# Head norms scaled by ScalarE out of the projection's bank, mixer outputs and K0 one step later in the order, the tanh table loaded behind the sines

## The chip, the core and the metric

The kernel runs on one core of a Trainium2 chip. The metric is the device time of one execution, in microseconds (us); the median of three runs counts. Five engines work in parallel, each through its own queue in order: TensorE (PE in the rows; its weight loads are PEld), VectorE (DVE), ScalarE (ACT), GpSimd (POOL) and SyncE (SP), which issues the DMA transfers. SBUF is the memory on the chip; PSUM holds the banks into which TensorE accumulates.

## What is computed

Two transformer blocks on 256 tokens of width 1024. The change touches the first block only: its input projections, and the two mixers that run beside them, a state space mixer and a sparse attention whose heads are normalized.

```python
def first_block(x, ...):
    h = rmsnorm(x, norm1_g[l])
    hp = h @ w_in[l]
    y_ssm = s5_mixer(hp[..., :o1], ...)
    y_nsa = nsa_mixer(hp[..., o1:o2], hp[..., o2:o3], hp[..., o3:o4], ...)
    gate = jax.nn.sigmoid(hp[..., o4:].reshape(bsz, s, N_MIXERS, D_MODEL))
    merged = gate[..., 0, :] * (y_ssm @ w_proj_ssm[l]) + gate[..., 1, :] * (y_nsa @ w_proj_nsa[l])
    x = x + merged @ w_out[l]
    ...                        # a feed-forward layer
def nsa_mixer(q, kv, ...):
    q = rmsnorm(q.reshape(bsz, s, G, HG, d), q_norm_g)      # 8 heads of 64, each with its own norm
    ks = rmsnorm(kv[1, 0], k_norm_g[1])                     # 2 of the 4 key heads
    kw = rmsnorm(kv[2, 0], k_norm_g[2])                     # the other 2
    ...
def s5_mixer(u, ...):
    bu = einsum(u, bbar); x = scan(abar, bu)                # complex states, 32 groups of 64
    y = einsum(x, c) + d * u; yg = gelu(y)
    return yg * sigmoid(yg @ w_glu + b_glu)
```

The second block (retention, latent attention, feed-forward layers) follows and is not changed.

## The kernel before

Tokens are two tiles of 128 (t = 0, 1), on the partitions of a projection's result. `block1_proj(t)` is a generator: it multiplies the unnormalized input `x32` by the weights of u, q, kvb, kva and mg one after the other, in PSUM banks (mm, acc0 to acc3), and each result is scaled by the token's norm factor `r` when it leaves its bank. q of tile t lies in bank acc{t}, kva of tile t in bank acc{2+t}. `head_norm` then squares the copy on ScalarE, sums each head's squares on VectorE, takes the power of -0.5 on GpSimd (`rsqrt`, line 332) and multiplies the copy by it on GpSimd (line 847). Its transposes come later, with the functions in `todo`, through the two banks `tr`.

The state space mixer goes in eight steps of `ssm_states(m)`, called s0 to s7: each is matmuls into acc0 and acc1, an evacuation by VectorE (line 754), and after a yield a scan (line 764), two products, and two combinations on GpSimd (lines 768, 769) into one of the three buffers X0 to X2. Line 731 on makes the tables that the steps need, from m = 1 on with GpSimd. Four outputs `ssm_out(i)`, called o0 to o3, read K0, the products `sC` and two of the X buffers, and end in a gelu on ScalarE and VectorE (lines 799, 554 to 557). `ssm_setup`, the generator `st`, makes the tables: sines (ScalarE's Sin table, then line 909's Tanh), the products `sC` (lines 627 to 629), K0 (32 matmuls of 32 columns, copied by line 698) and last the second half of `sC`.

The attention mixer `nsa_chain` compresses keys and values (64 small matmuls from buffers `XT`, which line 920 fills), and then goes through four pairs of heads (lines 1063 to 1084 and `nsa_values`).

What runs when is set in two places. `order` calls the generators D (projections of both tiles, one step apart), S (the mixer's steps), N (the attention) and st in an order written out by hand; `ssm_steps` holds the order of the mixer's steps as a string. From that program order a scheduler places the instructions on each engine's queue, where they then run in order; a wait for another engine's result stops the queue.

Of the kernel before, what the change touches and what calls it, by code (L numbers as in the profile page):

```python
# [12 lines left out]
AF = mybir.ActivationFunctionType  # L13
ALU = mybir.AluOpType
PSUM = bass.MemoryType.PSUM
P = 128
# [161 lines left out]
class Prog:  # L178
# [5 lines left out]
    def __init__(self, ctx, tc, ins, out):  # L184
        self.tc, self.nc, self.i, self.out, self.ctx = tc, tc.nc, ins, out, ctx
        self.dbg = {}
        ec = ctx.enter_context
        self.cp = ec(tc.tile_pool(name="cp", bufs=1))
        self.wp = ec(tc.tile_pool(name="wp", bufs=1))
        self.xp = self.np = None  # L190
        self.mrs = [None, None]
        self.un = 0
        self.hp = ec(tc.tile_pool(name="hp", bufs=1))
        self.pp = ec(tc.tile_pool(name="pp", bufs=1, space=PSUM))
        self.have, self.subs, self.copies, self.left = {}, {}, {}, {}
        keys = lambda *names: [key for name in names for key in UNITS if key[0] == name]
        mg = keys("mg")
        self.raws, self.seen, self.rn = keys("u", "q", "kvb", "kva") + mg[:2], set(), 0
        order = mg[2:]

        self.then = {mg[1]: mg[2]}
        self.ahead = dict(zip(order, order[1:]))
        self.n = 0
# [356 lines left out]
    def ssm_setup(self, pool, np_):  # L560
        nc, v, g = self.nc, self.nc.vector, self.nc.gpsimd
# [3 lines left out]
        def sb(s, tag):  # L565
            if list(s) != [P, 16]:
                return self.sb(pool, s, tag)
            used[0] += 1
            return small[:, used[0] - 1, :]
# [26 lines left out]
        sn, cs = e1[:, 1], e1[:, 0]  # L596
        yield
        self.sincos(pool, th, sn, cs, 16)

        def sq(o, x):  # L600
            t = self.sb(pool, [P, 2, 16], "q1", bufs=2)
            v.tensor_mul(t, x, x)
            v.tensor_sub(o[:, 0], t[:, 0], t[:, 1])
            v.scalar_tensor_tensor(o[:, 1], x[:, 0], 2.0, x[:, 1], op0=ALU.mult, op1=ALU.mult)
# [10 lines left out]
        abr, abi, nr = sb([P, 16], "abr"), sb([P, 16], "abi"), sb([P, 16], "nr")  # L615
# [167 lines left out]

    def ssm_steps(self, pool):
        st = [self.ssm_states(pool, m) for m in range(8)]
        for x in "s0 s1 s0 s2 s1 o0 s3 s2 s4 s3 o1 s5 s4 s6 s5 o2 s7 s6 s7 o3".split():
            i = int(x[1])
            if x[0] == "o":
                self.ssm_out(pool, i)
            else:  # L790
                next(st[i], None)
            yield
# [42 lines left out]
            nc.gpsimd.memset(self.XT[i][:, 256:], 0.0)  # L835
            nc.gpsimd.tensor_copy(self.XT[i][:, 256:272], pe[:, i, :])

    def head_norm(self, pool, src, n):
        nc, v = self.nc, self.nc.vector
        sq = self.sb(pool, [P, 2, 256], "ns1", bufs=2).rearrange("p a k -> p (a k)")  # L840
        nc.scalar.activation(sq[:, :n * 64], src, AF.Square, scale=0.125)
        ms = self.sb(pool, [P, 8], "nms", bufs=2)
        v.tensor_reduce(ms[:, :n], sq[:, :n * 64].rearrange("p (h d) -> p h d", h=n), axis=mybir.AxisListType.X, op=ALU.add)
        v.tensor_scalar_add(ms[:, :n], ms[:, :n], EPS)
        r = self.rsqrt(pool, ms[:, :n], n, tag="nr")
        s3 = src.rearrange("p (h d) -> p h d", h=n)
        nc.gpsimd.tensor_mul(s3, s3, r.unsqueeze(2).to_broadcast([P, n, 64]))

    def proj_then(self, out, name, n, hT, todo, after=1, raw=False):

# [7 lines left out]
    def block1_proj(self, sp, pool, t):  # L858

        nc, v = self.nc, self.nc.vector  # L860
        sq = self.sb(self.b1, [P, UW], "g8k", bufs=2)[:, :1024].rearrange("p (c t) -> p c t", c=8)
# [9 lines left out]
        r = self.rs[t] = self.norm_stats(pool, self.xT[t], f"rstd{t}", sq)  # L871
# [9 lines left out]
        pm = self.ps("mm")  # L881
# [8 lines left out]
        pm = self.ps(f"acc{t}")  # L890
        yield from self.proj_then(pm, "q", 0, x32, todo, 0, True)
        q = self.sb(pool, [P, 512], "q", bufs=2)
        nc.scalar.mul(q, pm, r)
        self.head_norm(pool, q, 8)

        def q_rest(q=q):
            x = flip(q, 4).rearrange("p (c t) -> p c t", c=4)
# [5 lines left out]
        pm = self.ps("mm")  # L903
# [19 lines left out]
        pm = self.ps(f"acc{2 + t}")  # L923
        yield from self.proj_then(pm, "kva", 0, x32, todo, 0, True)
        k = self.sb(pool, [P, 512], "q", bufs=2)[:, :256]
        nc.scalar.mul(k, pm[:, :256], r)
        nc.scalar.mul(self.V[:, t, :], pm[:, 256:], r)
        self.head_norm(pool, k, 4)

        def k_rest(k=k):  # L930
            pt = flip(k, 2)
# [8 lines left out]
        pm = self.ps("mm")  # L940
# [7 lines left out]
        for n in range(1, 4):  # L948
            pm = self.ps("mm")
# [198 lines left out]
    def order(self, D, st, S, N, sp):  # L1148

        next(D)  # L1150
        self.w1 = [self.sb(self.b1, [P, 16, P], "g8k", bufs=2) for _ in (0, 1)]
        for k in range(4):
            next(D)
            next(st)
            if k == 1:
                for i in (0, 1):
                    self.nc.sync.dma_start(self.w1[i], self.i["cw1"][i])
        next(S)
        next(D)
        next(st, None)  # L1160
        next(S)
        next(D)
        for k in range(2):
            for x in (S, N, S):
                next(x)
            next(st, None)
            next(D)
        while D is not None:
            for _ in range(3):
                next(S, None)  # L1170
                next(N, None)
            if next(D, 1) == 1:
                D = None
        self.weave(S, N)
# [474 lines left out]
```

## Time and profile before

| | |
|---|---|
| median of three runs | 1421.97 us (1418.32 to 1424.17) |
| the profiled execution | 1418.17 us, its span 1416.0 us |
| TensorE busy | 98% of the span |
| VectorE, ScalarE, GpSimd busy | 66%, 53%, 9% |
| mean granted TensorE clock | 0.995 of 2.4 GHz |

The span runs from the first to the last instruction; what lies around it makes up the rest of the execution's time. The first block takes about the first 220 us. Ends of matmuls are modelled in the profile, so that "busy" there means that TensorE had work, not that it was at its peak. A wait is idle time of an engine, put down to the instruction that came last.

### The profile page before, as it was taken

Reading aid. Unit: us, or ns where it says so; the run is one execution under the profiler, and the core shown is the slowest. Engines: PE = TensorE matmul, PEld = TensorE weight load, DVE = VectorE, ACT = ScalarE, POOL = GpSimd, SP = SyncE. Lnnn points to the kernel's source line nnn. Section 1 sums busy time; section 2 is a strip of 40 time slices with the busy share of each in tenths; the row PEclk is TensorE's granted clock in tenths of the full one; section 3 lists DMA queues with packets and bytes.
Section 4 is the critical chain, followed back from the end, with each engine's and each line's share of the span. In section 5 each row is a group of like instructions: output and inputs, shape, how many; then the busy total and the mean of one; then the engine's idle time right before and its main releaser. Section 6 shows DMA issues by size and latency. Waiting matters only on the chain.

```text
span 1416.0 us, 18450 instructions
## 1 busy us (share of the span) xinstructions
PE 1381.4 (98%) x6690; PEld 1107.7 (78%) x6690; DVE 928.5 (66%) x1990; ACT 749.3 (53%) x1647; POOL 129.8 (9%) x147
## 2 busy tenths in 40 slices
PE   7999999999999999999999999999999999999997
PEld 3656787888877888889877888878888887788886
DVE  6887687755676555587688565576555596865553
ACT  3345556544665444465366454465444576744442
POOL 1644100800000000011000000000000000000000
PEclk9998999999999999999999999999999999999999
DMA  9222355755545555435354555545555252565540
GB/s 359 87 91 68 109 208 180 251 189 180 178 179 192 194 179 180 152 104 194 127 199 158 182 211 188 181 146 208 188 198 179 81 180 81 187 212 197 186 149 30
DMA packets 39114, 238.62 MB, mean 169 GB/s; under 512 B 5744, under 2 KB 7024, under 8 KB 13424
## 3 DMA queue, kind: packets, MB, share of 16 engines
q1 hardware_dynamic: 39024, 237.45, 48.0%
q8 instruction: 52, 0.85, 0.2%
q14 instruction: 38, 0.31, 0.1%
HBM read 236.39 MB, written 1.05 MB: 168 GB/s over the span
## 4 chain that ended last, share of the span: by engine, by line
PE 78%; DVE 11%; ACT 3%; issue 3%; DMA 3%; POOL 2%; SPq 0%; POOLq 0%; DVEq 0%; ACTq 0%
PE mm L222 44%; PE acc L222 29%; PE tr L226 4%; DVE wl L263 3%; DMA raw<-in_wts_dram 3%; DVE s L375 2%; DVE hTl L390 1%; ACT wh L262 1%; PE tr L222 1%; DVE xT L430 1%; DVE tb L764 1%; ACT hTh L389 0%; POOL rr L332 0%; POOL nr L332 0%; DVE xT L426 0%
## 5 line engine op out<-in xcount | busy, mean ns | idle before, releaser
L263 DVE TENSOR_TENSOR wl<-raw,wh 128x512 fp32r<-128x512 f32 (+2 forms) x852 | 536.6, 681 | 255.6 <-ACT wh L262 254.9
L262 ACT CAST wh<-raw 128x512 fp32r<-128x512 f32 (+2 forms) x852 | 461.9, 606 | 303.5 <-PE mm L222 152.1
L222 PE MATMUL mm<-wh,hTl 128*128 128x512 f32 (+2 forms) x1056 | 406.1, 389 | 0.5 <-DVE hTl L390 0.5
L222 PE MATMUL mm<-wh,hTh 128*128 128x512 f32 (+2 forms) x1024 | 398.7, 390 | 2.3 <-ACT hTh L389 2.1
L222 PE MATMUL mm<-wl,hTh 128*128 128x512 f32 (+2 forms) x1024 | 393.6, 385 | 0.1
L222 PEld LDWEIGHTS mm<-wh,hTl 128*128 128x128 f32 x1056 | 198.9, 189 | 42.3 <-issue 3.4
L222 PEld LDWEIGHTS mm<-wh,hTh 128*128 128x128 f32 x1024 | 192.9, 188 | 42.9 <-ACT hTh L389 5.0
L222 PEld LDWEIGHTS mm<-wl,hTh 128*128 128x128 f32 x1024 | 193.0, 189 | 36.6 <-issue 0.7
L222 PE MATMUL acc<-wh,ffhh 128*128 128x512 f32 x480 | 196.4, 409 | 0.0
L222 PE MATMUL acc<-wh,ffhl 128*128 128x512 f32 x480 | 188.8, 393 | 0.0
L222 PE MATMUL acc<-wl,ffhh 128*128 128x512 f32 x480 | 188.7, 393 | 0.0
L449 ACT ACTIVATE ffs<-mm,rstd 128x256 f32<-128x256 f32 x88 | 41.7, 473 | 138.7 <-PE mm L222 137.9
L450 DVE SCALAR_TENSOR_TENSOR ffh<-mm,rstd,ffs 128x256 f32<-128x256 f32 x88 | 42.4, 482 | 104.1 <-ACT ffs L449 102.3
L222 PEld LDWEIGHTS acc<-wh,ffhl 128*128 128x128 f32 x480 | 90.2, 188 | 20.2
L222 PEld LDWEIGHTS acc<-wl,ffhh 128*128 128x128 f32 x480 | 90.6, 189 | 16.7
L222 PEld LDWEIGHTS acc<-wh,ffhh 128*128 128x128 f32 x480 | 90.3, 188 | 16.4
L332 POOL TENSOR_TENSOR rr<-ms,mhalf 128x1 f32<-128x1 f32 x12 | 7.1, 589 | 772.3 <-DVE ms L412 771.7
L222 PE MATMUL acc<-wh,mx 128*128 128x512 f32 x160 | 53.9, 403 | 0.1
L325 ACT CAST ffhh<-tr 128x256 fp32r<-128x256 f32 (+1 forms) x104 | 41.6, 400 | 20.7 <-PE tr L226 20.7
L326 DVE TENSOR_TENSOR ffhl<-tr,ffhh 128x256 fp32r<-128x256 f32 (+1 forms) x104 | 47.7, 459 | 6.1 <-ACT ffhh L325 5.3
L226 PE MATMUL tr<-idn,ffh 128*128 128x128 f32 x240 | 43.2, 272 | 0.0
L226 PEld LDWEIGHTS tr<-idn,ffh 128*128 128x128 f32 x240 | 32.2, 140 | 13.5 <-DVE ffh L450 0.6
(402 smaller groups left out, 1380.8 us busy)
## 6 DMA issues: line engine op xcount, KB each, us to landing
raw<-in_wts_dram SPq DMA_DIRECT2D x194, 1024.0 KB, 4.9
raw<-in_wts_dram SPq DMA_DIRECT2D x18, 768.0 KB, 4.2
raw<-in_wts_dram SPq DMA_DIRECT2D x4, 576.0 KB, 3.7
wl<-in_wts_dram SPq DMA_DIRECT2D x2, 1024.0 KB, 12.0
g8k<-in_cw_dram SPq DMA_DIRECT2D x2, 1024.0 KB, 10.0
wh<-in_wts_dram SPq DMA_DIRECT2D x2, 1024.0 KB, 9.1
memT<-in_memT_dram SPq DMA_DIRECT2D x4, 512.0 KB, 3.6
raw<-in_wts_dram SPq DMA_DIRECT2D x4, 256.0 KB, 5.7
```

Source lines behind the costliest of these rows:

```text
L222: self.nc.tensor.matmul(out, l, r, start=start, stop=stop, **kw)
L226: self.nc.tensor.transpose(out, src, self.idn[:n, :n])
L262: self.copies[key] = nc.scalar.copy(wh[:, s:s + h], raw[:, s:s + h]).ins
L263: self.subs[key] = nc.vector.tensor_sub(wl[:, s:s + h], raw[:, s:s + h], wh[:, s:s + h].bitcast(F32)).ins
L325: self.nc.scalar.copy(hi, src)
L326: self.nc.vector.tensor_sub(lo, src, hi.bitcast(F32))
L375: nc.vector.tensor_reduce(s8, sq.rearrange("p c t -> p t c"), axis=mybir.AxisListType.X, op=ALU.add)
L390: nc.vector.scalar_tensor_tensor(lo[:, c, :], xT[:, c, :], g[:, c:c + 1], hi[:, c, :].bitcast(F32), op0=ALU.mult, op1=ALU.subtract)
L430: nc.vector.scalar_tensor_tensor(xT[:, cc, :], pt[:, c * P:(c + 1) * P], gain[:, cc:cc + 1], xT[:, cc, :], op0=ALU.mult, op1=ALU.add)
L449: nc.scalar.activation(s, pm[:, :256], AF.Silu, scale=rstd)
L450: nc.vector.scalar_tensor_tensor(h, pm[:, 256:], rstd, s, op0=ALU.mult, op1=ALU.mult)
L764: v.tensor_tensor_scan(fb[:, n], RD.rearrange("p j t -> p (j t)"), fa[:, n], 0.0, op0=ALU.mult, op1=ALU.add)
```

## The change

Four things. `head_norm` now gets the bank: the Square reads it with the token's factor in its scale (`r8`), VectorE multiplies the heads' factors by `r` in a new row, and ScalarE writes each head out of the bank with one multiplication of 64 columns, in place of the copy and of GpSimd's multiplication. In the string of `ssm_steps` o0, o1 and o2 stand one step later. In `order` one `next(st, None)` is gone, so that K0 and the second half of `sC` each come one call later. And a one-column Tanh behind the sines brings in its table there.

```diff
@@ -596,6 +596,7 @@
         sn, cs = e1[:, 1], e1[:, 0]
         yield
         self.sincos(pool, th, sn, cs, 16)
+        self.table(AF.Tanh)
 
         def sq(o, x):
             t = self.sb(pool, [P, 2, 16], "q1", bufs=2)
@@ -783,7 +784,7 @@
 
     def ssm_steps(self, pool):
         st = [self.ssm_states(pool, m) for m in range(8)]
-        for x in "s0 s1 s0 s2 s1 o0 s3 s2 s4 s3 o1 s5 s4 s6 s5 o2 s7 s6 s7 o3".split():
+        for x in "s0 s1 s0 s2 s1 s3 o0 s2 s4 s3 s5 o1 s4 s6 s5 s7 o2 s6 s7 o3".split():
             i = int(x[1])
             if x[0] == "o":
                 self.ssm_out(pool, i)
@@ -835,16 +836,18 @@
             nc.gpsimd.memset(self.XT[i][:, 256:], 0.0)
             nc.gpsimd.tensor_copy(self.XT[i][:, 256:272], pe[:, i, :])
 
-    def head_norm(self, pool, src, n):
+    def head_norm(self, pool, out, src, n, r, r8):
+
         nc, v = self.nc, self.nc.vector
         sq = self.sb(pool, [P, 2, 256], "ns1", bufs=2).rearrange("p a k -> p (a k)")
-        nc.scalar.activation(sq[:, :n * 64], src, AF.Square, scale=0.125)
+        nc.scalar.activation(sq[:, :n * 64], src, AF.Square, scale=r8)
         ms = self.sb(pool, [P, 8], "nms", bufs=2)
         v.tensor_reduce(ms[:, :n], sq[:, :n * 64].rearrange("p (h d) -> p h d", h=n), axis=mybir.AxisListType.X, op=ALU.add)
         v.tensor_scalar_add(ms[:, :n], ms[:, :n], EPS)
-        r = self.rsqrt(pool, ms[:, :n], n, tag="nr")
-        s3 = src.rearrange("p (h d) -> p h d", h=n)
-        nc.gpsimd.tensor_mul(s3, s3, r.unsqueeze(2).to_broadcast([P, n, 64]))
+        nr = self.rsqrt(pool, ms[:, :n], n, tag="nr")
+        v.tensor_scalar_mul(nr, nr, r)
+        for h in range(n):
+            nc.scalar.mul(out[:, 64 * h:64 * h + 64], src[:, 64 * h:64 * h + 64], nr[:, h:h + 1])
 
     def proj_then(self, out, name, n, hT, todo, after=1, raw=False):
 
@@ -890,8 +893,9 @@
         pm = self.ps(f"acc{t}")
         yield from self.proj_then(pm, "q", 0, x32, todo, 0, True)
         q = self.sb(pool, [P, 512], "q", bufs=2)
-        nc.scalar.mul(q, pm, r)
-        self.head_norm(pool, q, 8)
+        r8 = self.sb(pool, [P, 1], "rn8", bufs=2)
+        v.tensor_scalar_mul(r8, r, 0.125)
+        self.head_norm(pool, q, pm, 8, r, r8)
 
         def q_rest(q=q):
             x = flip(q, 4).rearrange("p (c t) -> p c t", c=4)
@@ -923,9 +927,8 @@
         pm = self.ps(f"acc{2 + t}")
         yield from self.proj_then(pm, "kva", 0, x32, todo, 0, True)
         k = self.sb(pool, [P, 512], "q", bufs=2)[:, :256]
-        nc.scalar.mul(k, pm[:, :256], r)
         nc.scalar.mul(self.V[:, t, :], pm[:, 256:], r)
-        self.head_norm(pool, k, 4)
+        self.head_norm(pool, k, pm[:, :256], 4, r, r8)
 
         def k_rest(k=k):
             pt = flip(k, 2)
@@ -1157,7 +1160,6 @@
                     self.nc.sync.dma_start(self.w1[i], self.i["cw1"][i])
         next(S)
         next(D)
-        next(st, None)
         next(S)
         next(D)
         for k in range(2):
```

Three places show how the queues change. The first is VectorE, at the head norms of q (lines 842 to 844 before; `L845`, `L846`, `L848` in the changed file, whose numbers are two to three higher there). `nms` and `nr` are the heads' sums and factors, first of tile 0 and then of tile 1, and the `sC` rows are the products of the mixer's set-up. Before:

```order
L844 TENSOR_SCALAR nms_374<-nms_374 128x8
L627 TENSOR_TENSOR sC_403<-ns_79_319,small_152 128x512
L628 TENSOR_TENSOR ta_425<-V_142,small_152 128x512
L627 TENSOR_TENSOR sC_403<-ns_79_319,small_152 128x512
L629 TENSOR_TENSOR sC_403<-sC_403,ta_425 128x512
L628 TENSOR_TENSOR ta_429<-V_142,small_152 128x512
L627 TENSOR_TENSOR sC_403<-sC_403,small_152 128x512
L629 TENSOR_TENSOR sC_403<-sC_403,ta_429 128x512
L627 TENSOR_TENSOR sC_403<-sC_403,small_152 128x512
L843 TENSOR_REDUCE nms_414<-ns_104_412 128x8
L844 TENSOR_SCALAR nms_414<-nms_414 128x8
L754 TENSOR_TENSOR ta_443<-acc_110_433,cst_341 128x2x128
```

And now:

```order
L628 TENSOR_TENSOR sC_414<-ns_80_321,small_152 128x512
L848 TENSOR_SCALAR nr_98_380<-nr_98_380,rstd_19_125 128x8
L629 TENSOR_TENSOR ta_445<-V_142,small_152 128x512
L628 TENSOR_TENSOR sC_414<-ns_80_321,small_152 128x512
L630 TENSOR_TENSOR sC_414<-sC_414,ta_445 128x512
L629 TENSOR_TENSOR ta_449<-V_142,small_152 128x512
L628 TENSOR_TENSOR sC_414<-sC_414,small_152 128x512
L630 TENSOR_TENSOR sC_414<-sC_414,ta_449 128x512
L628 TENSOR_TENSOR sC_414<-sC_414,small_152 128x512
L845 TENSOR_REDUCE nms_426<-ns_107_424 128x8
L846 TENSOR_SCALAR nms_426<-nms_426 128x8
L848 TENSOR_SCALAR nr_109_429<-nr_109_429,rstd_51_201 128x8
```

Two rows came in, each of which reads GpSimd's power: one behind the first `sC` product, one between tile 1's sums and the evacuation of s0 (`ta<-acc`).

The second place is ScalarE at the same norms. acc_56 and acc_82 (acc_83 now) are the banks acc0 and acc1 with q of tile 0 and tile 1; mm is the bank of kvb. Before:

```order
L893 ACTIVATE q_370<-acc_56_212,rstd_19_125 128x512
L841 ACTIVATE ns_94_372<-q_370 128x512
L893 ACTIVATE q_410<-acc_82_330,rstd_51_201 128x512
L681 COPY sB_76_299<-tr_391 128x4x128
L681 COPY sB_76_299<-tr_397 128x4x128
L841 ACTIVATE ns_104_412<-q_410 128x512
L758 COPY RD_40_169<-small_152 128x2x127
L908 ACTIVATE q_454<-mm_380,rstd_19_125 128x256
L909 ACT_TABLE_LOAD
```

And now:

```order
L843 ACTIVATE ns_96_375<-acc_56_212,rn_95_373 128x512
L850 ACTIVATE q_372<-acc_56_212,nr_98_380 128x64 x8
L843 ACTIVATE ns_107_424<-acc_83_332,rn_106_422 128x512
L682 COPY sB_77_301<-tr_402 128x4x128
L682 COPY sB_77_301<-tr_408 128x4x128
L850 ACTIVATE q_421<-acc_83_332,nr_109_429 128x64 x8
L759 COPY RD_40_169<-small_152 128x2x127
L912 ACTIVATE q_474<-mm_391,rstd_19_125 128x256
L913 ACTIVATE gts_143<-mm_391,hr_472 128x24
```

The last read of acc0 and acc1 is now that of the eight pieces, which need the `nr` rows above; the table load has gone from this place to behind the sines.

The third place is VectorE between the first two pairs of heads (lines 1069 to 1077 before, 1072 to 1080 now), at the evacuation of s6 (line 754 before, 755 now; it needs a `cst` table of GpSimd). Before:

```order
L1077 TENSOR_TENSOR ns_255_1130<-ns_255_1130,nsm_1117 128x256
L1070 TENSOR_TENSOR nsm_1121<-nsm_1121,gts_143 128x4
L765 TENSOR_TENSOR ta_1092<-tb_1093,cst_1073 128x512
L754 TENSOR_TENSOR ta_1246<-acc_271_1236,cst_1227 128x2x128
L754 TENSOR_TENSOR tb_1247<-acc_271_1236,cst_1227 128x2x128
L754 TENSOR_TENSOR ta_1246<-acc_272_1237,cst_1227 128x2x128
L754 TENSOR_TENSOR tb_1247<-acc_272_1237,cst_1227 128x2x128
L1077 TENSOR_TENSOR ns_256_1135<-ns_256_1135,nsm_1121 128x256
```

And now:

```order
L1080 TENSOR_TENSOR ns_258_1156<-ns_258_1156,nsm_1143 128x256
L1072 RECIPROCAL nsm_1147<-nsm_1147 128x4
L766 TENSOR_TENSOR ta_1078<-tb_1079,cst_1059 128x512
L1073 TENSOR_TENSOR nsm_1147<-nsm_1147,gts_143 128x4
L767 TENSOR_TENSOR tb_1079<-tb_1079,cst_1059 128x512
L1080 TENSOR_TENSOR ns_259_1161<-ns_259_1161,nsm_1147 128x256
L263 TENSOR_TENSOR wl_1363<-raw_1361,wh_1362 128x512
L755 TENSOR_TENSOR ta_1272<-acc_274_1262,cst_1253 128x2x128
```

The second product of the pair now stands ahead of the evacuation of s6. On TensorE, of what the text below speaks of, K0's 32 matmuls moved from ahead of s1 to behind the compression's matmuls, s3 moved from behind tile 1's k transposes to ahead of them, and o0 from ahead of mg's first matmuls to behind these transposes; s0 stands where it stood.

## Rows read from the trace of the kernel before

**Rows 1.** The page: busy times (part 1), GpSimd's one-column powers (part 5).

```profile
PE 1381.4 (98%) x6690; PEld 1107.7 (78%) x6690; DVE 928.5 (66%) x1990; ACT 749.3 (53%) x1647; POOL 129.8 (9%) x147
...
L332 POOL TENSOR_TENSOR rr<-ms,mhalf 128x1 f32<-128x1 f32 x12 | 7.1, 589 | 772.3 <-DVE ms L412 771.7
```

**Rows 2.** TensorE's waits, 0 to 160 us: us in total, times, longest.

```profile
PE tr L226 <- DVE ns L1077: 2.3, 2, 1.8
PE tr L226 <- POOL q L847: 1.8, 1, 1.8
PE tr L222 <- DVE qT L900: 1.6, 1, 1.6
PE tr L226 <- DVE s L994: 0.8, 1, 0.8
...
PE acc L222 <- DVE tb L754: 0.4, 1, 0.4
```

**Rows 3.** Busy times by stretch; behind them the granted clock and DMA.

```profile
92.00:146.00 54.00, 49.97 (x317) 34.89 (x317) 45.21 (x147) 31.49 (x99) 21.58 (x25) 0.91 0.24 76
```

**Rows 4.** Timeline of TensorE: start, duration, line, operation, count [idle before <-releaser].

```profile
45.04 1.16 PE L222 MATMUL acc<-uT,sB 32*128 32x128 f32 x16
...
53.94 0.76 PE L222 MATMUL tr<-sC,PT 128*32 128x32 f32 x64 [1.57 <-DVE qT L900]
```

**Rows 5.** Timeline of VectorE at the q norms.

```profile
37.17 1.23 DVE L627 TENSOR_TENSOR sC<-ns,small 128x512 f32<-128x512 f32 x1
...
43.74 0.68 DVE L627 TENSOR_TENSOR sC<-sC,small 128x512 f32<-128x512 f32 x1
44.35 0.67 DVE L843 TENSOR_REDUCE nms<-ns 128x8 f32<-128x512 f32 x1
45.05 0.30 DVE L844 TENSOR_SCALAR nms<-nms 128x8 f32<-128x8 f32 x1
```

**Rows 6.** Timeline of GpSimd: table products and the powers of the q norms.

```profile
39.98 2.09 POOL L733 TENSOR_TENSOR cstt<-BA 128x256 f32<-128x256 f32 x2
42.03 2.10 POOL L332 TENSOR_TENSOR nr<-nms,mhalf 128x8 f32<-128x8 f32 x1
...
45.43 1.65 POOL L332 TENSOR_TENSOR nr<-nms,mhalf 128x8 f32<-128x8 f32 x1
...
55.54 1.21 POOL L733 TENSOR_TENSOR cstt<-BA 128x256 f32<-128x256 f32 x2
```

**Rows 7.** Timeline of ScalarE: behind the sines, the table load, copies of 64 columns.

```profile
27.93 0.69 ACT L884 ACTIVATE q<-mm,rstd 128x512 f32<-128x512 f32 x1 [6.66 <-PE mm L222]
...
50.95 1.28 ACT L909 ACT_TABLE_LOAD   x1
...
54.28 0.42 ACT L920 COPY XT<-tr 64x64 f32<-64x64 f32 x2 [0.81 <-DVE XT L920]
```

**Rows 8.** Timeline: a k norm's power, s4 on TensorE, a cast on ScalarE.

```profile
69.86 4.33 POOL L332 TENSOR_TENSOR nr<-nms,mhalf 128x4 f32<-128x4 f32 x1 [2.91 <-DVE nms L844]
...
90.10 1.79 PE L222 MATMUL acc<-uT,sB 32*128 32x128 f32 x16 [0.41 <-DVE tb L754]
...
90.86 0.62 ACT L262 CAST wh<-raw 128x512 fp32r<-128x512 f32 x1 [1.96 <-DMA raw<-in_wts_dram]
```

**Rows 9.** VectorE's wait at s6 (timeline), and three stretches as in rows 3.

```profile
128.48 0.42 DVE L754 TENSOR_TENSOR ta<-acc,cst 128x256 f32<-128x256 f32 x1 [1.78 <-POOL cst L734]
...
130.00:132.00 2.00, 1.26 (x8) 1.20 (x9) 2.00 (x8) 0.81 (x3) 0.29 (x1) 0.86 0.00 0
132.00:134.00 2.00, 2.00 (x8) 1.16 (x8) 2.00 (x10) 2.00 (x10) 1.99 (x3) 0.50 0.00 0
134.00:136.00 2.00, 2.00 (x16) 1.46 (x14) 0.66 (x2) 0.39 (x3) 2.00 (x3) 0.78 0.00 0
```

**Rows 10.** Timeline of TensorE at the start.

```profile
7.15 2.05 PE L222 MATMUL mm<-raw,hTl 128*128 128x512 f32 x2 [7.15 <-DMA raw<-in_wts_dram]
...
13.28 3.60 PE L222 MATMUL mm<-wh,hTl 128*128 128x512 f32 x8
```


## The prediction

> **What bounds the kernel now.** I read the page's busy shares first: TensorE is busy for 1381.4 us of the 1416.0 us span [rows 1], so a change on other engines is worth only what it takes from, or adds to, TensorE's waits and its clock. The list of TensorE's waits over the first 160 us, where all the edits lie, comes next. Besides the first load it holds five groups that the edits touch: 2.3 us on `L1077` (two, the longest 1.8), 1.8 on `L847`, 1.6 on `L900`, 0.8 on `L994`, 0.4 on `L754` [rows 2]. Last I read busy time and granted clock by stretch: from 92 to 146 us the mean clock is 0.91 [rows 3], that is 54 × 0.09 × 2 = 9.7 us at 1.2 GHz where the rest runs at 2.4. So the most that perfect order could give is some 7 us of waits and 5 us of clock. Half a per cent of the time, about what a measurement of this kernel can tell from no change, is 7.1 us.
>
> **The change, part by part.** *The norms.* Before, ScalarE copied a projection out of its bank in one instruction (`L893`), and GpSimd scaled the copy (`L847`). Now the Square reads the bank, VectorE scales the 8 (or 4) factors by `r`, and ScalarE takes each head out of the bank by a multiplication of its own. Two things follow that the diff doesn't show.
>
> First, VectorE gets a row (`L848`) that waits for GpSimd's power, and its queue stops there. For token tile 0 it stands one row behind the first `sC` product, with seven products of K0's set-up, the other tile's reduce and the evacuation of s0 behind it. VectorE comes to it at 37.17 + 1.23 = 38.4. GpSimd began that power at 42.03 [rows 5, 6], behind table products that it must still do first. Between 38.4 and 42.03 it worked through some 3.5 products at about 1.05 us each, against VectorE's, of which one took 1.23 instead of 0.61. Alone it takes 0.60 for one [rows 6], so with VectorE at rest the power starts near 40.6, takes the 1.65 of the second power, and with its signal and the scaling row VectorE goes on at about 42.6 (estimates from these rows, as all that follows). Seven products at 0.61 (from 43.74 to 44.35) lead to 46.9, the reduce at 0.70 to 47.6, the small row to 47.8, the second power at 1.65 to 49.45, its `L848` to 49.7 [rows 5, 6].
>
> Second, the bank is held until its last head is out. The q projections of the tiles lie in acc0 and acc1, and s0 of the state space part writes the same two banks. Before, they were free by then, and TensorE ran s0 at 45.04 without waiting [rows 4]. Now the second matmul of s0 needs the eight pieces of tile 1, which start at 49.7. The nearest row is the pair of 64x64 copies out of a bank, 0.42 for two [rows 7], so eight take 1.7. That leads to 51.5 with the signal: **TensorE waits 6.5 us more at s0**, and everything behind is in order on TensorE.
>
> *A page on that price.* The Trainium skill, ScalarE: Activation LUTs, section "What ACT_TABLE_LOAD costs", gives an activation with one pointer operand 280 ns and 0.833 ns an element, and an overlap of 93 ns between two; eight of 64 would be 2.0 us, an estimate from that page. It speaks against cutting one instruction into eight, and by it the wait would be 6.8. No row here has just this form, so the copies' 0.21 stands.
>
> The bounds of the 6.5: the power of one column takes 0.589 in the mean [rows 1], so two powers can't save more than 2.1 (4.4 us); the first power took 2.10, and two such and slower pieces add 1.3 (7.8 us).
>
> *K0 one step later, the tanh table earlier.* K0's matmuls waited 1.57 us for `L900` [rows 4], which stood behind the 1.28 us table load on ScalarE [rows 7]. The load goes to 21.3 us, where ScalarE idles 6.66 us [rows 7], and costs nothing; without that cover it would cost 1.28 on the u copy. K0 now runs behind the compression's matmuls. **−1.6**; nothing takes the place of this wait, since the copy `L908` and the transposes that need it both move with s0.
>
> *The k norms.* `L847` made TensorE wait 1.8 us because the power in front of it took 4.33 us beside a busy VectorE [rows 2, 8]. Now the k norm of tile 0 starts as soon as its bank is done, VectorE stands still for its power, and 64 matmuls of the compression and K0 lie before its transposes: **−1.8**.
>
> *Outputs one step later.* s3 now comes ahead of o0, so that s3 and s4 no longer stand back to back. There s4 waited 0.41, and its 16 matmuls took 1.79 instead of 1.16 [rows 4, 8]: **−1.0**. Before, the chain to `L994` stood on ScalarE behind a cast that waited 1.96 us for its load [rows 8]; now that cast comes after it: **−0.8**. Between 124 and 131 us the second `L1077` stood behind an `L754` that waited 1.78 us for a GpSimd table [rows 9]; now it stands ahead of it: **−1.8**, the longest of these waits [rows 2].
>
> *The clock.* After the first load, 7.15 us of idling, the first 8 matmuls of 512 columns took 6.1 us (7.15 to 13.28), the next 8 took 3.60 [rows 10]: 2.5 us lost. After the wait of 1.8 us on `L1077` the granted clock was 0.86, 0.50 and 0.78 in three stretches of 2 us [rows 9], 3.4 us at 1.2 GHz, 1.7 lost. A wait of 6.5 us lies between these, nearer the first: **+2.0** (0 to 2.5). With the wait on `L1077` goes the fall behind it: **−1.7**. The first fall of that stretch, 9.7 − 3.4 = 6.3 us long, stays: it doesn't hang on the wait on `L1077`, which comes behind it.
>
> *Unseen.* VectorE has five more rows and four stops. The nearest danger is tile 1's k norm, whose transposes come about 0.6 us behind its heads, with o0's `sC` behind the same stop: **+1.0** (0 to 2.7, the difference of a power at 4.33 and one at 1.65 [rows 6, 8]).
>
> **The sum**: 6.5 − 1.6 − 1.8 − 1.0 − 0.8 − 1.8 + 2.0 − 1.7 + 1.0 = **+0.8 us**. The profiled execution took 1418.17 (span 1416.0, and 2.2 around it) and would go to 1419.0. It lies 3.8 under the median of the three runs, 1421.97, so the forecast for a median is 1422.8, no change that can be measured.
>
> **The rivals.** *VectorE doesn't catch up (slower).* Stopped four times in order, it stays behind from s0 on; the waits on `L994` and `L1077` and the fall of the clock, which all come from its being late, stay (0.8 + 1.8 + 1.7 = 4.3), and the power of tile 1's k norm runs at 4.33 against VectorE's products (2.7 in place of 1.0). Sum: 0.8 + 4.3 + 1.7 = 6.8, or 1428.8. For it: VectorE was busy 45.21 of 54 us there [rows 3], and the change takes no work from it. Against: s3's scans come earlier than before. It decides from 6.3 us beyond the sum on, where the loss passes 7.1.
> A page beside it: the Trainium skill, SBUF — State Buffer, section "SBUF: two separate sides", says that a VectorE instruction with two inputs in SBUF and a GpSimd one hold the port that they share in turn, each for a whole instruction. The 4.33 us power agrees with that [rows 8]; by this rule the case is the nearer, the more of VectorE's products lie beside a norm's power.
>
> *The wait at s0 isn't there (faster).* If the heads were out of acc1 before 45, only the removed waits would count: 0.8 − 6.5 − 2.0 = −7.7, or 1414.3. That needs both powers done 6 us sooner; GpSimd's in-order table products [rows 6] speak against it.
>
> *The order around 107 us changes the first fall too.* Its 6.3 us cost 3.1. Without it the time is 1419.7. The new order there puts wide matmuls between narrow ones, at places that the rows can't weigh.
>
> **How the numbers follow.** The sum's case gets 0.62, with a range of its own from 1418 to 1426 (the bounds of the wait, of the clock and of the unseen, taken partly together). Lateness gets 0.18, no wait 0.08, the lost fall 0.12. Slower by over 0.5% is half of the lateness case (0.09) and the far tail of the sum's (0.04), 0.13; faster by over 0.5% is most of the no-wait case (0.06) and a little of the lost fall (0.02), 0.08; the rest, 0.79, is within 0.5%. The range 1415.5 to 1430 reaches to both neighbours and leaves out most of the no-wait case and the tail beyond lateness.
>
> **What would show it.** In the trace after: TensorE waiting 4.4 to 7.8 us on ScalarE's head pieces at s0, near 45; VectorE idle about 4 us before its first `L848`, with GpSimd as releaser; a lower clock right behind 51; no wait on `L900` or on the k heads of tile 0; transposes near 75 about 3 us later than before, and those after 131 level with before. I am wrong if TensorE passes 45 without a wait, if VectorE isn't stopped by the power, or if the stretch from 92 to 146 us keeps its waits or gets new ones.

## The result and the profile after

The changed kernel takes 1434.57 us in the median (1432.29 to 1436.29), the kernel before 1421.6 in the same rounds: a ratio of 1.0097 [1.0082, 1.0112], 13 to 14 us slower, and outside the predicted range. The profiled execution took 1435.47 us with a span of 1433.5, 17.5 more than the span of before; that one lay some 3 us under its median, so the traces differ by more than the medians. TensorE runs the same 6690 instructions by tile and shape; what differs is waits and clock. In the lists of the changed kernel line numbers are up to 3 higher (`L1077` is now `L1080`, `L994` is `L997`, `L1036` is `L1039`).

TensorE's waits over the first 160 us of the changed kernel, to be held against [rows 2]:

```profile
engine line waited for: us in total, times, longest us
PE mm L222 <- DMA raw<-in_wts_dram: 7.9, 1, 7.9
PE acc L222 <- ACT q L850: 5.4, 1, 5.4
PE tr L226 <- DVE cs L1039: 1.9, 1, 1.9
PE tr L222 <- DVE kT L939: 1.9, 1, 1.9
PE tr L222 <- POOL cst L735: 1.9, 1, 1.9
PE tr L226 <- ACT ns L1078: 1.6, 1, 1.6
PE tr L226 <- DVE ns L1080: 1.3, 1, 1.3
PE acc L222 <- ACT sB L682: 0.8, 1, 0.8
PE tr L226 <- DVE s L997: 0.6, 1, 0.6
```

The waits on `L900`, on the k heads and on `L754` are gone; the wait at s0 is there; and five of 1.3 us and more stand in the list behind it, of which before had only `ns` on VectorE at such a length. Next the granted clock by stretch (busy time and rows of each engine, then clock, DMA share and GB/s), where before had 1.00, 0.91 [rows 3] and 1.00:

```profile
45.00:92.00 47.00, 38.95 (x262) 23.79 (x261) 31.75 (x71) 17.99 (x53) 19.25 (x26) 0.85 0.17 58
92.00:146.00 54.00, 46.68 (x276) 30.61 (x275) 44.27 (x140) 25.55 (x77) 16.06 (x18) 0.88 0.22 72
146.00:160.00 14.00, 13.55 (x79) 9.29 (x77) 12.21 (x37) 9.08 (x28) 6.62 (x9) 0.87 0.29 95
```

That is 47 × 0.15 × 2 + 54 × 0.12 × 2 + 14 × 0.13 × 2 = 30.7 us at 1.2 GHz, where before had 9.7 [rows 3]. TensorE does half as much in such a microsecond, so 21.0 more of them cost 10.5. Added up over stretches of 1 us the two kernels have 30.7 and 10.2, in four falls (50 to 58, 74 to 82, 118 to 130, 142 to 150 us) against two. **So between these two executions 10 of the 17.5 us are clock, 7.6 are TensorE's waits, and 0.8 is the first load**: 18.4, about what is to be explained. Between the medians the share of the clock is smaller, some 4 us of 13, because the profiled execution of before had a higher clock than most of its others; the part "Kernel or execution?" below has the numbers.

The place of the s0 product in the changed kernel, on TensorE (start, duration, instructions, idle time before and its releaser), on ScalarE, on VectorE and on GpSimd:

```profile
46.83 0.48 PE L222 MATMUL acc<-uT,sB 32*128 32x128 f32 x2 [0.80 <-ACT sB L682]
52.71 2.07 PE L222 MATMUL acc<-uT,sB 32*128 32x128 f32 x14 [5.40 <-ACT q L850]
54.71 5.04 PE L222 MATMUL acc<-raw,hTl 128*128 128x512 f32 x8
...
74.04 0.44 PE L222 MATMUL tr<-g8k,XT 128*48 128x128 f32 x2 [1.85 <-POOL cst L735]
```
```profile
43.97 1.75 ACT L850 ACTIVATE q<-acc,nr 128x64 f32<-128x64 f32 x8 [11.06 <-DVE nr L848]
50.91 1.75 ACT L850 ACTIVATE q<-acc,nr 128x64 f32<-128x64 f32 x8 [3.65 <-DVE nr L848]
```
```profile
43.65 0.23 DVE L848 TENSOR_SCALAR nr<-nr,rstd 128x8 f32<-128x8 f32 x1 [4.88 <-POOL nr L332]
50.65 0.23 DVE L848 TENSOR_SCALAR nr<-nr,rstd 128x8 f32<-128x8 f32 x1 [1.76 <-POOL nr L332]
72.06 0.58 DVE L848 TENSOR_SCALAR nr<-nr,rstd 128x4 f32<-128x4 f32 x1 [2.25 <-POOL nr L332]
72.56 0.45 DVE L924 COPY XT<-tr 64x64 f32<-64x64 f32 x2
73.03 0.75 DVE L904 SCALAR_TENSOR_TENSOR qT<-tr,g,qT 128x512 fp32r<-128x512 f32 x1
```
```profile
69.75 0.73 POOL L770 TENSOR_TENSOR X<-tb,ta 128x256 f32<-128x256 f32 x1
70.43 0.62 POOL L733 TENSOR_TENSOR cst<-BA 128x256 f32<-128x256 f32 x1
71.01 1.02 POOL L332 TENSOR_TENSOR nr<-nms,mhalf 128x4 f32<-128x4 f32 x1
```

VectorE stops 4.88, 1.76 and 2.25 us for the powers, the eight pieces come out of the bank in 1.75, and TensorE loses 0.80 + 5.40 at s0. The eight matmuls behind take 5.04 us; before, at the full clock, they took 3.70:

```profile
46.13 3.70 PE L222 MATMUL acc<-raw,hTl 128*128 128x512 f32 x8
```

At 72 us the stop for k's power makes the `XT` copies and the `qT` product late, which stand right behind it on VectorE. TensorE's wait of 1.85 at 74 is put down to a table row of GpSimd that ended last, but TensorE goes on 0.26 us after the `qT` product ends (73.78 to 74.04). In e3 and e11 below the distance is the same (0.26 and 0.25), and in e11 the profile names that product. So it is VectorE's stop that shows there.

### The profile page after: what moved, and what is told of

Same layout as the page of the kernel before. It is cut to its first block, busy times and chain, and to the rows that moved or that the text cites. A ratio compares the mean times of both kernels' runs of the same rounds, so it can differ in the third digit from the quotient of the medians.

```text
span 1433.5 us, 18463 instructions
## 1 busy us (share of the span) xinstructions
PE 1391.1 (97%) x6690; PEld 1112.3 (78%) x6690; DVE 929.8 (65%) x1996; ACT 755.9 (53%) x1668; POOL 121.1 (8%) x143
## 4 chain that ended last, share of the span: by engine, by line
PE 79%; DVE 11%; DMA 3%; ACT 3%; issue 2%; POOL 2%; SPq 0%; POOLq 0%; DVEq 0%; ACTq 0%
PE mm L222 44%; PE acc L222 30%; PE tr L226 4%; DMA raw<-in_wts_dram 3%; DVE wl L263 3%; DVE s L375 1%; PE tr L222 1%; DVE hTl L390 1%; ACT wh L262 1%; DVE xT L430 1%; ACT hTh L389 0%; POOL nr L332 0%; POOL cst L733 0%; DVE xT L426 0%; DVE tb L765 0%
```

## The experiments

**Theory A**: the norms, by the held bank and by VectorE's stops, cause nearly all of the loss; later waits and the falls of the clock follow from them. **Rival B**: the order edits cause it. **Rival C**: the clock falls wherever narrow matmuls and short waits meet, whatever the norms do. All ratios are to the kernel before. "Waits" is TensorE's idle time before 175 us without that for the first load; "low" the time at 1.2 GHz between 28 and 400 us, added up over stretches of 1 us; both, and "span", are of the one profiled execution. "Clock" is the mean granted clock as a share of 2.4 GHz: the median of all executions, and in brackets that of the profiled one.

| kernel | ratio | waits | low | span | clock |
|---|---|---|---|---|---|
| before | 1 | 8.5 | 10.2 | 1416.0 | 0.991 (0.995) |
| after | 1.0097 [1.0082, 1.0112] | 16.1 | 30.7 | 1433.5 | 0.988 (0.988) |
| e1 norms alone | 1.0071 [1.0052, 1.0091] | 14.9 | 34.1 | 1432.0 | 0.988 (0.987) |
| e2 order edits alone | 1.0013 [0.9998, 1.0027] | 7.8 | 23.9 | 1420.3 | 0.9895 (0.989) |
| e3 q in other banks | 1.0059 [1.0037, 1.0082] | 12.9 | 30.7 | 1430.0 | 0.9885 (0.988) |
| e4 scaling on GpSimd | 1.0063 [1.0042, 1.0083] | 13.1 | 30.7 | 1429.0 | 0.988 (0.988) |
| e5 = e3 and e4 | 1.0021 [1.0002, 1.0039] | 10.1 | 20.4 | 1424.3 | 0.991 (0.990) |
| e9, e9b s0's wait filled | 1.0105, 1.0094 | 9.9, 10.0 | 27.3, 30.6 | 1434.5, 1433.6 | 0.989, 0.989 (0.988, 0.988) |
| e10 only q changed | 1.0066 [1.0047, 1.0084] | 12.4 | 34.1 | 1429.5 | 0.9885 (0.986) |
| e11 only k changed | 1.0041 [1.0026, 1.0057] | 10.0 | 30.8 | 1426.9 | 0.989 (0.988) |
| e6 string alone | 1.0056 [1.0040, 1.0073] | 11.2 | 27.3 | 1424.3 | 0.9885 (0.988) |
| e8 tanh table alone | 1.0001 [0.9987, 1.0014] | 6.9 | 17.0 | 1417.4 | 0.992 (0.992) |
| e13 q only, both remedies | 1.0037 [1.0021, 1.0052] | 11.3 | 10.2 | 1420.1 | 0.9925 (0.995) |
| e14 pieces from the copy | 1.0043 [1.0024, 1.0061] | 12.1 | 6.8 | 1418.9 | 0.990 (0.996) |

In every row without added matmuls the waits, half of the low time and the first load explain the span's difference to within some 3 us.

**Norms or order.** e1 is the changed kernel with these three edits taken back; e2 is the kernel before with them:

```diff
+        self.table(AF.Tanh)
...
-        for x in "s0 s1 s0 s2 s1 o0 s3 s2 s4 s3 o1 s5 s4 s6 s5 o2 s7 s6 s7 o3".split():
+        for x in "s0 s1 s0 s2 s1 s3 o0 s2 s4 s3 s5 o1 s4 s6 s5 s7 o2 s6 s7 o3".split():
...
-        next(st, None)
```

> Takes the changed kernel and puts the order string, the place of K0 and the load of the tanh table back as before: the head norms on ScalarE alone. Theory A (the norms hold the projection's bank and make VectorE stop on GpSimd's power; the falls of the clock and the later waits follow): 8 to 13 us slower than before (ratio 1.006 to 1.009), a wait of TensorE of about 6 us at the s0 product, at least 20 us at the lower clock before 160 us. Rival B (the order edits cause the loss): within 3 us of before. Rival C (only the mix of narrow matmuls decides the clock): a loss of 4 to 8 us, with the s0 wait there.

> Takes the kernel before and makes the three other edits alone: mixer outputs one step later in the string, K0 one step later, the tanh table brought in behind the sines; the head norms stay on VectorE. Theory A: 0 to 3 us faster than before (1.6 for K0 and about 1.0 for the s4 wait, by the waits of [rows 2]), no wait of over 1 us at the s0 product. Rival B (the order edits cause the loss): 8 to 13 us slower. Rival C: within 4 us of before on either side, with falls of the clock at other places.

e1 loses 10 us, with 5.40 + 0.84 at s0 and 34.1 us of low clock; e2 loses 2, at most 4. B falls; A holds for the bulk. But e2 was expected by A to gain, and its profile shows why it doesn't: the waits on `L900` and `L994` are gone, that on `ns` is shorter, yet

```profile
PE tr L226 <- POOL q L848: 2.4, 1, 2.4
PE tr L226 <- DVE cs L1037: 1.9, 1, 1.9
PE tr L222 <- ACT PT L1085: 1.2, 1, 1.2
```

new waits take their place: all in all e2 waits 7.8 us, 0.7 less than before. The wait on `cs` comes with the order edits, not with VectorE's stops: it is 1.9 here and 0.4 in e1. The low clock is 23.9 us in this execution against 10.2; over all executions the two kernels are nearer (0.9895 and 0.991, some 2 us of cost).

**The two harms apart.** The first pair of lines is e3, the second e4; e5 has both.

```diff
-        pm = self.ps(f"acc{t}")
+        pm = self.ps(f"acc{2 + t}")
...
-        v.tensor_scalar_mul(nr, nr, r)
+        nc.gpsimd.tensor_scalar_mul(nr, nr, r)
```

> The changed kernel with the q projections put into two other accumulator banks, so that the banks that the s0 product wants are not held until ScalarE has scaled the heads. Theory A: the wait at s0 falls from 6.2 to below 1.5 us, the first fall of the clock (48 to 57 us) is gone, the time is within 4 us of before. Rival B: ratio unchanged near 1.009. Rival C: the s0 wait is gone but the falls at 72, 116 and 140 us stay, at least 15 us at the lower clock, and the time stays 6 us or more above before.

> The changed kernel with the small product of the norm's root and the weight (128x8 or 128x4) given to GpSimd, right behind its power, so that VectorE no longer stops for that power; the banks are still held. Theory A, with both parts of the norms to blame: the wait at s0 falls only to about 4 us, the waits at 74 and later shrink by half, 5 to 9 us slower than before. If VectorE's stops are the whole cause: within 2 us of before. If the held bank is the whole cause: still 11 to 14 us slower. Rival B: unchanged near 1.009.

> Both at once in the changed kernel: the q projections in banks that s0 does not want, and the small product of root and weight on GpSimd, so that VectorE does not stop for the power. Theory A (the two parts of the norms together are the whole loss): no wait at s0, the waits behind 60 us as in the kernel before, within 3 us of before. Rival C (the clock falls wherever TensorE meets narrow matmuls and short waits, and moves with any change of the order): still 4 to 9 us slower, with 20 us or more at the lower clock.

In e3 the wait at s0 and the fall behind it are gone, as A had it, but the time is 8.4 us above before, outside A's 4, and the low clock is the same 30.7 us at other places: that was C's forecast. VectorE's stops stay (2.24 us for k's power), and TensorE waits 2.8 us ahead of the `XT` transposes. In e4 the wait on the heads falls to 3.9, but one of 2.4 on the sB copies joins it, so that the second part of s0 starts at 51.91, only 0.8 earlier than in the changed kernel; later waits shrink, and 9.0 us is the upper end of A's range. With both (e5) the time is 3.0 us above before (0.3 to 5.5). The remedies give 5.4 and 4.8 alone and 10.8 together, each known to about 3 us: **bank and stops are some 11 of the 14 us**, 6.0 of it TensorE's waits and some 4 the clock (0.988 to 0.991). A holds in the main and not in all: e5 lies at the edge of A's 3 us, its 20.4 us of low clock is what C named, and there is still a wait at s0. What e5 keeps is on ScalarE, where the pieces stand ahead of the copies that s0 needs, and TensorE waits 2.4 us for them:

```profile
45.15 1.75 ACT L850 ACTIVATE q<-acc,nr 128x64 f32<-128x64 f32 x8 [12.66 <-POOL nr L848]
46.74 0.74 ACT L843 ACTIVATE ns<-acc,rn 128x512 f32<-128x512 f32 x1
47.31 1.13 ACT L682 COPY sB<-tr 128x512 f32<-128x512 f32 x2
```

**q or k.** Both keep the order edits; e10 has the k norms as before (`head_norm_old` is the function of before), e11 the q norms:

```diff
+        nc.scalar.mul(k, pm[:, :256], r)
         nc.scalar.mul(self.V[:, t, :], pm[:, 256:], r)
-        self.head_norm(pool, k, pm[:, :256], 4, r, r8)
+        self.head_norm_old(pool, k, 4)
```

> The changed kernel, order edits included, with the k norms as before (ScalarE's copy of the k half, GpSimd's scaling) and only the q norms on ScalarE. Theory A with the q norms to blame (bank, 6 us wait, fall behind it): 7 to 12 us slower than before. If the k norms carry half: 3 to 6 us slower.

> The changed kernel, order edits included, with the q norms as before and only the k norms on ScalarE. Theory A with the q norms to blame: 0 to 4 us slower than before, no wait of over 1 us at s0. If the k norms carry half: 5 to 8 us slower, through the wait of TensorE near 74 us on the copies behind VectorE's stop and the later waits.

Against e2, q costs 7.5 us (1.0066 to 1.0013) and k 4.0, each give or take 3. With the 1.8 of e2 that is 13.3, near the 13.8 of the whole change. e10 lies in the range for the q norms to blame; e11, 5.8 us above before, lies above its range for that and in the one for the k norms carrying half. The k norms, which I had at a gain, lose. In e11 VectorE stands 2.25 us for the power, and TensorE waits 2.8 for the `qT` product behind it, where before lost 1.8 on the k heads; the low clock is 30.8 us:

```profile
61.13 0.43 DVE L857 TENSOR_SCALAR nms<-nms 128x4 f32<-128x4 f32 x1
63.80 0.58 DVE L859 TENSOR_SCALAR nr<-nr,rstd 128x4 f32<-128x4 f32 x1 [2.25 <-POOL nr L332]
64.30 0.45 DVE L936 COPY XT<-tr 64x64 f32<-64x64 f32 x2
64.78 0.75 DVE L916 SCALAR_TENSOR_TENSOR qT<-tr,g,qT 128x512 fp32r<-128x512 f32 x1
```
```profile
65.78 0.64 PE L222 MATMUL tr<-g8k,XT 128*48 128x128 f32 x2 [2.76 <-DVE qT L916]
```

**Does filling the wait keep the clock?** e9 and e9b put twelve and six matmuls into acc0 ahead of s0; all other orders are those of the changed kernel. This is e9; in e9b the same line runs six times:

```diff
         bu = [self.ps("acc0"), self.ps("acc1")]
+        if m == 0:
+            for c in range(12):
+                self.mm(bu[0], self.idn, self.xT[0][:, 4 * (c % 2):4 * (c % 2) + 4, :].rearrange("p c t -> p (c t)"), True, True)
```

> The changed kernel with twelve matmuls of 128x512 into bank acc0 ahead of the s0 product (s0 writes the bank anew, so nothing is changed in the result), 5.5 us by 0.46 each: they fill the wait for the heads of tile 1 with work. Order on every engine is otherwise that of the changed kernel. If the wait is what brings the clock down behind it: no clock of 0.50 between 48 and 58 us and 3 to 4 us faster than the changed kernel (ratio to before 1.006 to 1.007). If the clock falls there for another reason: the lower clock stays, no gain, 0 to 1 us slower than the changed kernel. If the waits later on hang on this delay alone they stay, as the delay does.

> The changed kernel with six matmuls of 128x512 ahead of the s0 product in place of twelve: the run before took 10.46 us for its twelve, so six take 5.2 us and end no later than the heads are out. If the fall of the clock behind s0 costs what it takes from TensorE there: no clock of 0.50 between 48 and 58 us, s0's second half at 52 to 53 us as in the changed kernel, and 1.5 to 3.5 us faster than the changed kernel (ratio 1.007 to 1.009). If VectorE's and GpSimd's chains set the time up to 75 us, so that the fall lay in the shadow of the next wait: TensorE's wait near 74 us grows by about 1.5 us, and less than 1 us is won.

Twelve took 10.46 us, not 5.5 (a matmul of this type is two rows of the trace), so s0 came at 55.46, 2.75 us after its second part in the changed kernel, and nothing was to be won in time. But the wait at s0 was gone, and with it the fall behind s0: the granted clock is 1.00 from 44 to 64 us, and the eight matmuls behind take 3.70 again:

```profile
45.07 10.46 PE L222 MATMUL acc<-xT,idn 128*128 128x512 f32 x24
55.46 1.16 PE L222 MATMUL acc<-uT,sB 32*128 32x128 f32 x16
56.55 3.70 PE L222 MATMUL acc<-raw,hTl 128*128 128x512 f32 x8
```

Other falls came further on, and the sum was 27.3 us. Six fitted:

```profile
45.20 5.31 PE L222 MATMUL acc<-xT,idn 128*128 128x512 f32 x12
50.45 0.48 PE L222 MATMUL acc<-uT,sB 32*128 32x128 f32 x2
51.82 1.15 PE L222 MATMUL acc<-uT,sB 32*128 32x128 f32 x14 [0.89 <-ACT q L856]
52.90 5.40 PE L222 MATMUL acc<-raw,hTl 128*128 128x512 f32 x8
```

A wait of 0.89 us is left at s0, and the clock still fell behind it, for 3.4 us (53 to 57) in place of 6.8; a new fall stood at 101 to 108, the sum stayed at 30.6, and the time at 1.0094 [1.0076, 1.0113]. So a fall right behind s0 goes with the long wait there, as A says: the changed kernel in both its profiles, e1, e4 and e10, with 6 us of waiting, all have one, and e3, e5, e9 and e13, with 0 to 2.4 us, have none. But that fall doesn't decide the sum, and mending it bought nothing: against A's simple chain, for C.

**The order edits apart.** e6 has the string line of e2 alone, e8 the `table` line alone; K0's move has no run of its own.

> The kernel before with the new string alone (mixer outputs one step later). As the prediction had it: waits on the s4 product, L994 and the second ns transposes gone, 4 to 5 us faster with the second fall of the clock. If what the string frees goes into a new wait on the compression's chain (cs L1036, 1.9 us in the run with all order edits) and into longer falls: the lower clock covers 17 us or more before 160 us, and the time lies within 3 us of before.

> The kernel before with the tanh table brought in behind the sines alone: the order on all engines but ScalarE's table loads is that of before. If the table load of 1.28 us makes K0's matmuls wait: the wait of 1.57 us on L900 falls below 0.4 us and the time falls by 0 to 2 us (ratio 0.9985 to 1.000). If K0 waits for something else there: the wait stays at 1.2 us or more, and the time is that of before within 1 us.

e6 loses 8 us (the rival's 3 are passed too): the compression's `L994` stands on VectorE behind a power for 3.45 us, and TensorE waits 3.4 us for it:

```profile
98.69 0.70 DVE L994 TENSOR_TENSOR s<-s,nr 16x128 f32<-16x128 f32 x1 [3.45 <-POOL nr L332]
```

With K0 and the table moved as well (e2) 6 of these come back. In e8 only ScalarE's table loads differ in order, and K0's wait falls from 1.57 to 0.15, as predicted. The time is that of before within 2 us on either side, so a gain of 1.6 is neither shown nor excluded. In the profiled execution the clock falls for 6.8 us where in that of before it didn't:

```profile
88.00:92.00 4.00, 3.58 (x29) 2.93 (x28) 2.83 (x12) 2.00 (x6) 0.00 (x0) 0.90 0.34 143
92.00:96.00 4.00, 4.00 (x11) 2.81 (x11) 2.89 (x12) 1.33 (x5) 0.69 (x1) 0.50 0.00 0
96.00:100.00 4.00, 4.00 (x20) 3.19 (x18) 1.81 (x8) 0.49 (x2) 0.00 (x0) 0.75 0.02 4
```

Both profiles of e8 have this fall and neither of before has it, so it may be the edit's. But a lower clock in sum is not shown: over all executions e8's is 0.992 in the median, and that of before in the same rounds 0.992 as well.

**Kernel or execution?** Second profiles:

> The kernel before, profiled a second time. If places and lengths of the lower clock belong to the kernel and its order: falls at 107 to 115 and 131 to 135 us again, about 10 us in all. If they belong to the execution: other places, or more than 3 us apart in all.

> The changed kernel, profiled a second time. If the lower clock belongs to the kernel: four falls again near 50, 74, 118 and 142 us, 28 to 33 us in all. If it belongs to the execution: a sum between 10 and 25 us, at other places.

> The kernel with the tanh table alone moved, profiled a second time. If the fall near 91 us belongs to its order and waits: there again. If to the execution: gone, or elsewhere.

The unchanged files once more. Before has 10.3 us of low clock (109 to 116, 133 to 137), the changed kernel 30.6 in four falls (47 to 58, 75 to 79, 116 to 127, 139 to 147), the tanh kernel 17.0 with the fall at 91 to 99 again. The waits repeat too (8.8 and 15.5 us, against 8.5 and 16.1). By two profiles of each the sums seem to belong to the kernel.

The granted clock of all executions says otherwise for before. In the 74 executions measured beside these experiments it runs from 0.988 to 0.997, with 0.991 in the median, and only 18 of them reach 0.994. Both profiles of before (0.995 and 0.994) are such executions; most others spent more time at 1.2 GHz, 0.991 being 1419 × 0.009 × 2 = 25.5 us of the whole span, some 4 of them, in every profile, at its end. The changed kernel lies between 0.986 and 0.990, with 0.988 in the median: 1432 × 0.012 × 2 = 34.4 us. So from median to median the change brings 8.9 us more at 1.2 GHz and not 20.5, an estimated cost of 4.4 us; with 7.6 us of waits that makes 12.0 of the 13.0 us. The low column of the table compares single executions, and differences of 10 us in it can be those of two executions of one kernel.

**Better versions.**

> The changed kernel with the k norms as before, the q norms on ScalarE, the q projections in banks that s0 does not want and the small product on GpSimd. If the q norms' loss is the held bank and VectorE's stop and no more: 0 to 3 us slower than before, as the order edits alone were. If ScalarE's sixteen pieces cost of themselves (the sB copies that s0 needs stand behind them): still 3 to 7 us slower, with a wait of 2 us or more on the sB copy at s0.

> The kernel before with the tanh table brought in behind the sines and with GpSimd's scaling of the heads replaced by ScalarE's pieces, taken from the copy of the projection and scaled by the root alone: ScalarE does the pieces, but the bank is free after the copy and VectorE has no row behind GpSimd's power. If bank and stop are the whole harm: the wait on the k heads near 75 us falls below 1 us and the time is within 2 us of before on either side. If sixteen and eight pieces cost on ScalarE of themselves: 3 us or more slower, with waits on ScalarE's rows behind them.

e13 joins e10 with the lines of e3 and e4. e14 is e8 with the scaling of ScalarE's copy given to ScalarE:

```diff
-        nc.gpsimd.tensor_mul(s3, s3, r.unsqueeze(2).to_broadcast([P, n, 64]))
+        for h in range(n):
+            nc.scalar.mul(s3[:, h, :], s3[:, h, :], r[:, h:h + 1])
```
```profile
45.00 2.02 ACT L849 ACTIVATE q<-q,nr 128x64 f32<-128x64 f32 x8 [11.45 <-POOL nr L332]
46.93 0.67 ACT L895 ACTIVATE q<-acc,rstd 128x512 f32<-128x512 f32 x1
47.50 1.05 ACT L682 COPY sB<-tr 128x512 f32<-128x512 f32 x2
```

e13 (5.3 us slower, 3.0 to 7.4) and e14 (6.1, 3.4 to 8.7) lie above the bounds without such a cost, e13 just so: ScalarE's pieces cost of themselves. TensorE waits 2.4 and 2.2 us for the sB copies behind them, and in e14 the k heads still make it wait 2.8. Their profiled executions were faster than their medians (e14's span of 1418.9 against a median time of 1427.5), so their low clock in the table is that of a short execution. Over all executions e13's clock (0.9925) is no lower than that of before, so its loss is not clock. e5, which is e13 with the new k norms, was not slower than it (1.0021 and 1.0037): without VectorE's stop the k norms show no cost, which fits the stop as its cause. No version beat the kernel before.

## Why the prediction was wrong, point by point

The forecast for a median was 1422.8 us, 0.8 above before; measured were 13.0. The step that failed is that removed waits were counted as gone: the terms for waits come to +0.5 us (6.5 − 1.6 − 1.8 − 1.0 − 0.8 − 1.8 + 1.0), and TensorE's waits grew by 7.6, since others took the places of those removed. The second is the size of the clock's term: +0.3 (2.0 − 1.7), against an estimated 4.4 between the medians and 10.2 between the two profiled executions.

- *The wait at s0, +6.5*: right in mechanism and size. 5.40 for the heads, and 0.80 ahead of them for the sB copies behind tile 0's pieces, which the forecast did not have; VectorE idle 4.88 ahead of its first `L848`, pieces 1.75 against the 1.7 from [rows 7]. The 2.0 from the Trainium skill (ScalarE: Activation LUTs, section "What ACT_TABLE_LOAD costs") was too high for pieces out of a bank; from an SBUF copy, in e14, eight took 2.02, which agrees.
- *K0, −1.6*: the wait went (0.15 in e8). *s4, −1.0*: went too.
- *k norm, −1.8, and unseen, +1.0*: **failed**. "VectorE stands still for its power" was taken as harmless; but the stop has the `XT` copies and the `qT` product behind it, and the wait moved to them. Measured, the k norms cost +4.0 us, give or take 3. The power itself took 1.02 beside a resting VectorE against 4.33 beside its products [rows 8]. That agrees with the port rule that the prediction cites from the Trainium skill (SBUF — State Buffer, section "SBUF: two separate sides"). The power got faster beside a VectorE that stood, and the late rows of VectorE cost more than that.
- *`L994`, −0.8, and the second `L1077`, −1.8*: **failed**. 0.6 stays on `L997`; 1.3 and 1.6 stand at `ns`, and 1.9 each on `L939` and `L1039`, which were 0 and 0.4. VectorE was late, which was the slower rival; its price of 6.8 us was half of what came. But the stops are not the only cause: e2, which has none of the new stops, already waits 1.9 for `cs` and 1.1 for `ns` on ScalarE, and e1, which has them without the order edits, waits 0.4 and nothing there. Of the 5.2 us of waits that the order edits were to remove, 0.7 were won in e2. The transposes near 75, forecast 3 us later, stand at 86.14, 11 later, and the end of the stretch isn't level with before but 18 us behind.
- *The clock, +2.0 − 1.7*: **failed in size**. A fall right behind s0 came, 6.8 us long or 3.4 of cost against the 2.0, and so far the mechanism was right: in e9, without the wait, it is gone. But the term priced one new fall and took one old one away, where the trace has 20.5 us more at 1.2 GHz, 10.2 us of cost, and the medians 8.9, some 4.4 of cost. The old falls and their lengths were read from one execution of before, which had a higher clock than most. The order edits, predicted at −6.9 with their waits and the second fall, measured +1.8 (−0.3 to +3.8).
- What stays open: which rows make the clock fall, and why executions of the same kernel differ in it. In the traces falls follow waits of 1.2 us and more at many places, but not at all (before's `L847`), and in e8 one came without a wait of over 0.5 us near it.

## What to carry to other kernels

An instruction that waits for another engine's result in the middle of an in-order queue is priced by what stands behind it, not by its own time; a bank is held until its last reader, so cutting one evacuation into pieces behind a long chain delays whoever reuses the bank. A removed wait is won only when what stands behind it has been followed to the next wait: here 5.2 us of removed waits left 0.7 in e2. And the granted clock in a profile is that of one execution: executions of the unchanged kernel ran from 1414 to 1426 us, and their clocks from 0.988 to 0.997, so before a fall of the clock is put down to an edit, the clocks of many executions of both kernels are to be compared.

## What was unexpected of the hardware

Executions of the same kernel differed in granted clock: the nine of before with 0.997 have spans of 1412 to 1414 us, the one with 0.988 has 1423. Twelve matmuls in the place of a 5.4 us wait kept the clock up behind them (e9); six, with 0.89 us of waiting left, did not (e9b, 3.4 us at 1.2 GHz in place of 6.8), and in neither did the time fall. Eight ScalarE pieces of 128x64 took 1.75 us out of the bank and 2.02 out of SBUF.
